# Attention weights times values: one F32 product on each column half of TensorE, in place of two split products

## The chip, the core and the metric

One core of a Trainium2 chip runs the whole kernel. Its engines work side by side and wait for each other on semaphores: PE (TensorE, the matrix unit; PEld is its loading of the stationary operand), DVE (VectorE), ACT (ScalarE), POOL (GpSimd), SP (SyncE, which issues most transfers) and the DMA engines. The metric is the device time of one execution in microseconds, the median of several runs.

## The reference, cut to what matters

The layer has three token mixers; the change touches the first, sparse attention with 8 heads of 64 in 2 groups, over 512 tokens in blocks of 128. With 8 blocks of 64 tokens and a top-k of 16, every block is selected, so the "selected" and the "window" attention are both plain causal attention, each with its own keys and values. What is computed per query block, cut down:

```python
p_c = _masked_softmax(einsum('bqghd,bngd->bghqn', qblk, k_cmp), valid_c)
o_c = einsum('bghqn,bngd->bqghd', p_c, v_cmp)
...
p_s = _masked_softmax(einsum('bqghd,bgqkd->bghqk', qblk, k_sel), valid_s)
o_s = einsum('bghqk,bgqkd->bqghd', p_s, v_sel)
...
p_w = _masked_softmax(einsum('bqghd,bkgd->bghqk', qblk, kwb), valid_w)
o_w = einsum('bghqk,bkgd->bqghd', p_w, vwb)
return gblk[..., 0:1] * o_c + gblk[..., 1:2] * o_s + gblk[..., 2:3] * o_w
```

The change is about the three products with the values, `o_c`, `o_s` and `o_w`.

## The kernel before, in words

Nearly all products run on float32r operands. No operand is used rounded alone; each is split in two: a high part (`wh`, `hH`, `ysH`, `ph`), which is the operand rounded to float32r by a copy, and a low part (`wl`, `hL`, `ysL`, `pl`), which is the rest and takes a subtraction. A full product is then three matmuls, high by high, high by low and low by high. `fm_block` and `tm_chunk` do this for the big projections: they load weights (`wr`), split them (`wh` on ACT in line 78, `wl` on DVE or POOL in line 79), and run three matmuls for each of 4 or 8 row blocks into a PSUM tile `mm_ps`. Every matmul is issued by the helper `mm` and so has line 62.

Attention is the loop over `ATT = (3, 2, 1, 0)`, the query blocks from the longest to the shortest. For each block `i` it makes compressed scores for the 8 heads (`sc_c`, softmax in `pcm`). Then for each group `g` of 4 heads:

- `o_ps`, one PSUM bank of 128 x 512, collects the output. It has one buffer (`BO = 1`).
- The compressed weights are transposed (`pc_ps`, line 836), spread over the four heads (`pd`, line 840, DVE), split into `ph` (line 843, ACT) and `pl` (line 844, DVE), and multiplied with `vcst`.
- For each of the two branches `b`: four heads of scores (`s_ps`), the row maximum (`mx`, line 858, DVE), the exponential (line 859, ACT), and the scaling of `P` (lines 865 and 867, on ACT, DVE or POOL). Then for each key tile `kt` up to `i`: four transposes of `P` into `p_ps` (line 872, two buffers), the split into `ph` (line 875, ACT) and `pl` (line 876, DVE), and two matmuls into `o_ps`.

The values are stationary. `vst` holds, side by side, the high part of the values in columns 0 to 63 and the low part in columns 64 to 127. So one matmul with `ph` and all 128 columns gives high by high in partitions 0 to 63 and high by low in partitions 64 to 127, and a second with `pl` and columns 0 to 63 adds low by high. Afterwards line 881 copies the lower half out (ACT), and line 885 adds both halves and puts the heads where the next stage wants them, `nsaY` (DVE, two instructions).

There are 40 such key tiles over all blocks, groups and branches (each of `i + 1` tiles, 2 groups, 2 branches) and 8 compressed products, 48 in all.

Instructions of each engine run in an order that the framework fixes when the program is built; it lays the work out on a simulated timeline, so an edit in one place can shift the order elsewhere. Between the steps of attention it puts the matmuls of `merge(1, ...)` and `merge(2, ...)`, which mix the other two branches into `macc` through `fm_block` (`mm_ps` from `ysH`, `ysL` or `hH`, `hL`). `HOLD` keeps the last four units of `merge(2, ...)` until certain products of attention are done (`anch`).

Of the kernel before, what the change touches and what calls it, by code (L numbers as in the profile page):

```python
# [9 lines left out]
F32 = mybir.dt.float32  # L10
R = mybir.dt.float32r
# [14 lines left out]
BS = 3  # L26
BO = 1
BP = 2
PS = "VVSG"
ATT = (3, 2, 1, 0)  # L30
HOLD = (-1,) * 12 + (3, 4, 5, 6)
# [9 lines left out]
def f(ap):  # L41
    return ap.bitcast(F32)
# [3 lines left out]
def hybrid_kernel(ctx, tc, x, p, norm_g, w_in, cmp_w1, cmp_w2, cmp_pe, sg_ln_g, sg_ln_b, sg_w, sg_b,  # L46
# [14 lines left out]
    def mm(o, a, b, start, stop, **kw):  # L61
        return PE.matmul(o, a, b, start=start, stop=stop, **kw).ins  # L62
# [173 lines left out]
    stp = st_ctx.enter_context(tc.tile_pool(name="stp", bufs=2))  # L236

    kcst = const.tile([128, 2, 2, 32], R, name="kcst")
    vcst = const.tile([128, 2, 128], R, name="vcst")
    hm = const.tile([128, 4], F32, name="hm")  # L240
    G.memset(hm, 0.0)
    for hh in range(4):
        G.memset(hm[32 * hh:32 * hh + 32, hh:hh + 1], 1.0)
    cp_ctx = ExitStack()
    cpp = cp_ctx.enter_context(tc.tile_pool(name="cpp", bufs=1))
    cps = cp_ctx.enter_context(tc.tile_pool(name="cps", bufs=1, space=PSUM))
# [60 lines left out]
    for kv in range(2):  # L307
        slp = slp2[:, kv * 64:kv * 64 + 64]
        sl = cpp.tile([128, 2, 4, 32], F32, tag=f"sl{kv}", name="sl")
        if kv == 0:  # L310
            sl = sl[:, 0, 0:2, :].rearrange("p g n -> p (g n)")
            V.tensor_copy(sl, slp)
            pk = cps.tile([128, 64], F32, tag="pk", name="pk")
            mm(pk, w2t[:, 0, :], sl, True, True)
            pk2 = pk.rearrange("p (g n) -> p g n", g=2)
            S.activation(kcst[:, :, 0, :], pk2, AF.Copy, scale=0.5)
            V.scalar_tensor_tensor(kcst[:, :, 1, :], pk2, 0.5, f(kcst[:, :, 0, :]), op0=OP.mult, op1=OP.subtract)
        else:
            V.tensor_copy(sl, slp.rearrange("p (g n) -> p g n", g=2).unsqueeze(2).to_broadcast([128, 2, 4, 32]))
            for g in range(2):  # L320
                pk = cps.tile([128, 64], F32, tag="pk", name="pk")
                mm(pk, sl[:, g].rearrange("p a n -> p (a n)"), w2t[:, 1, 0:64], True, True)
                S.activation(vcst[:, g, 0:64], pk, AF.Copy, scale=0.5)
                V.scalar_tensor_tensor(vcst[:, g, 64:128], pk, 0.5, f(vcst[:, g, 0:64]),
                                       op0=OP.mult, op1=OP.subtract)


    sh_ctx = ExitStack()
# [397 lines left out]
    nsa = nsa_ctx.enter_context(tc.tile_pool(name="nsa", bufs=1, side="right"))  # L726
    qst = nsa.tile([128, 4, 2, 512], R, name="qst")
    kst = [nsa.tile([128, 2, 2, 512], R, name=f"kst{b}") for b in range(2)]
    vst = nsa.tile([128, 4, 2, 2, 128], R, name="vst")
    nanch = []  # L730
    gate = nsa.tile([128, 4, 24], F32, name="gate")

# [1 line left out]

    def ev_v(t, ps):
        pv = ps[:, 0:256].rearrange("p (b g d) -> p b g d", b=2, g=2)
        S.copy(vst[:, t, :, :, 0:64], pv)
        V.tensor_tensor(vst[:, t, :, :, 64:128], pv, f(vst[:, t, :, :, 0:64]), OP.subtract)
        a_ = S.activation(gate[:, t, :], ps[:, 256:280], AF.Tanh, scale=0.5).ins
        nanch.append((a_, V.tensor_scalar(gate[:, t, :], gate[:, t, :], 0.5, 0.5, op0=OP.mult, op1=OP.add).ins))  # L740
    tm_chunk([(w_in, O_NVS, 128), (w_in, O_NVW, 152)], hH, hL, 8, ev_v)
# [69 lines left out]
    for i in ATT:  # L811
        isl = slice(i * 128, (i + 1) * 128)
        W = (i + 1) * 128
        sc = aps.tile([128, 8, 64], F32, tag="pt", name="sc_c", bufs=BP)
        for h in range(8):
            mm(sc[:, h, :], qst[:, h // 2, h % 2, isl], kcst[:, h // 4].rearrange("p a n -> p (a n)"), True, True)
        pcm = ap_.tile([128, 8, 32], F32, tag="pcm", name="pcm")
        mx8 = ap_.tile([128, 8], F32, tag="mx8", name="mx8")
        sm8 = ap_.tile([128, 8], F32, tag="sm8", name="sm8")
        V.tensor_tensor(pcm, sc[:, :, 0:32], cmask[:, i:i + 1, :].to_broadcast([128, 8, 32]), OP.add)  # L820
        V.tensor_tensor(pcm, sc[:, :, 32:64], pcm, OP.add)
        V.tensor_reduce(mx8, pcm, axis=AX.X, op=OP.max)
        V.tensor_tensor(pcm, pcm, mx8.unsqueeze(2).to_broadcast([128, 8, 32]), OP.subtract)
        S.activation(pcm, pcm, AF.Exp)
        V.tensor_reduce(sm8, pcm, axis=AX.X, op=OP.add)
        V.reciprocal(sm8, sm8)
        gv = gate[:, i, :].rearrange("p (h b) -> p b h", b=3)
        if i == 0:
            V.scalar_tensor_tensor(sm8, sm8, rowm, gv[:, 0, :], op0=OP.mult, op1=OP.mult)
        else:  # L830
            V.tensor_tensor(sm8, sm8, gv[:, 0, :], OP.mult)
        V.tensor_tensor(pcm, pcm, sm8.unsqueeze(2).to_broadcast([128, 8, 32]), OP.mult)
        for g in range(2):
            o_ps = aps.tile([128, 512], F32, tag="o", name="o_ps", bufs=BO)
            pc_ps = aps.tile([128, 128], F32, tag="pt", name="pc_ps", bufs=BP)
            PE.transpose(pc_ps, pcm[:, 4 * g:4 * g + 4, :].rearrange("p h n -> p (h n)"), ident)
            pd = ap_.tile([128, 4, 128], F32, tag="pd", name="pd", bufs=1)
            ph = ap_.tile([128, 512], R, tag="ph", name="ph", bufs=3)
            pl = ap_.tile([128, 512], R, tag="pl", name="pl", bufs=3)
            V.tensor_tensor(pd, pc_ps.unsqueeze(1).to_broadcast([128, 4, 128]),  # L840
                            hm.unsqueeze(2).to_broadcast([128, 4, 128]), OP.mult)
            pd2 = pd.rearrange("p h t -> p (h t)")
            S.copy(ph, pd2)
            V.tensor_tensor(pl, pd2, f(ph), OP.subtract)
            mm(o_ps, vcst[:, g, :], ph, True, False)
            mm(o_ps[0:64], vcst[:, g, 0:64], pl, False, False)
            for b in range(2):
                P = ap_.tile([128, 4, 512], F32, tag="P", name="P")
                mx = ap_.tile([128, 4], F32, tag="mx", name="mx")
                sm = ap_.tile([128, 4], F32, tag="sm", name="sm")  # L850
                for hh in range(4):
                    h = g * 4 + hh
                    s_ps = aps.tile([128, 512], F32, tag="s", name="s_ps", bufs=BS)
                    qs = qst[:, h // 2, h % 2, isl]
                    mm(s_ps[:, :W], qs, kst[b][:, g, 0, :W], True, False)
                    mm(s_ps[:, :W], qs, kst[b][:, g, 1, :W], False, False)
                    mm(s_ps[:, i * 128:W], identb, trib, False, True)
                    V.tensor_reduce(mx[:, hh:hh + 1], s_ps[:, :W], axis=AX.X, op=OP.max, negate=True)  # L858
                    S.activation(P[:, hh, :W], s_ps[:, :W], AF.Exp, bias=mx[:, hh:hh + 1],  # L859
                                 accum_out=sm[:, hh:hh + 1])  # L860
                V.reciprocal(sm, sm)
                V.tensor_tensor(sm, sm, gv[:, 1 + b, g * 4:g * 4 + 4], OP.mult)
                for hh in range(4):
                    if PS[hh] == "S":
                        S.activation(P[:, hh, :W], P[:, hh, :W], AF.Copy, scale=sm[:, hh:hh + 1])
                    else:
                        (G if PS[hh] == "G" else V).tensor_scalar(P[:, hh, :W], P[:, hh, :W], sm[:, hh:hh + 1],
                                                                  None, op0=OP.mult)
                for kt in range(i + 1):
                    p_ps = aps.tile([128, 512], F32, tag="pt", name="p_ps", bufs=BP)  # L870
                    for hh in range(4):
                        PE.transpose(p_ps[:, hh * 128:hh * 128 + 128], P[:, hh, kt * 128:kt * 128 + 128], ident)  # L872
                    ph = ap_.tile([128, 512], R, tag="ph", name="ph", bufs=3)
                    pl = ap_.tile([128, 512], R, tag="pl", name="pl", bufs=3)
                    S.copy(ph, p_ps)  # L875
                    V.tensor_tensor(pl, p_ps, f(ph), OP.subtract)  # L876
                    mm(o_ps[0:64], vst[:, kt, b, g, 0:64], pl, False, False)
                    last = mm(o_ps, vst[:, kt, b, g, :], ph, False, b == 1 and kt == i)
            anch.append(last)
            ot = ap_.tile([64, 512], F32, tag="ot", name="ot", bufs=1)  # L880
            S.copy(ot, o_ps[64:128])
            o4 = o_ps.rearrange("p (a e t) -> p a e t", a=2, e=2)
            t4 = ot.rearrange("p (a e t) -> p a e t", a=2, e=2)
            for e in range(2):
                V.tensor_tensor(nsaY[e * 64:e * 64 + 64, 2 * g:2 * g + 2, isl], o4[0:64, :, e, :], t4[:, :, e, :],
                                OP.add)
    at_ctx.close()
    nsa_ctx.close()

# [118 lines left out]
```

## Time and profile before

| | us |
|---|---|
| median of 3 runs (745.38 to 746.82) | 745.41 |
| the profiled execution | 747.35 |
| its span (first to last instruction) | 745.6 |
| PE busy in the span | 716.0 |
| DVE, ACT, POOL busy | 407.6, 354.2, 288.2 |
| attention with the merges in between, 395.6 to 566.3 | 170.7 |

The page of the profile has busy time by engine, the span in 40 slices (each digit the busy share in tenths, the row PEclk the clock that TensorE was granted), the DMA queues, the chain of work that ended last, and the costliest groups of instructions. A group reads: line, engine, operation, what is written from what, its shape, its count, busy time and mean, then idle time before it with what ended that. Matmuls overlap in a pipeline, so a recorded length is longer than the step from one start to the next; what a matmul costs the engine is read from the starts.

### The profile page before, as it was taken

Reading aid. Unit: us, or ns where it says so; the run is one execution under the profiler, and the core shown is the slowest. Engines: PE = TensorE matmul, PEld = TensorE weight load, DVE = VectorE, ACT = ScalarE, POOL = GpSimd, SP = SyncE. Lnnn points to the kernel's source line nnn. Section 1 sums busy time; section 2 is a strip of 40 time slices with the busy share of each in tenths; the row PEclk is TensorE's granted clock in tenths of the full one; section 3 lists DMA queues with packets and bytes.
Section 4 is the critical chain, followed back from the end, with each engine's and each line's share of the span. In section 5 each row is a group of like instructions: output and inputs, shape, how many; then the busy total and the mean of one; then the engine's idle time right before and its main releaser. Section 6 shows DMA issues by size and latency. Waiting matters only on the chain.

```text
span 745.6 us, 13074 instructions
## 1 busy us (share of the span) xinstructions
PE 716.0 (96%) x4941; PEld 606.6 (81%) x4941; DVE 407.6 (55%) x775; ACT 354.2 (48%) x743; POOL 288.2 (39%) x276
## 2 busy tenths in 40 slices
PE   4899999999999999999999999989999999999995
PEld 4788788999878987779877778767877888998995
DVE  6531587758933773645676565397554222226345
ACT  6554555542372332234565554576554333227453
POOL 6444740120220272300144345323445565256563
PEclk9999999999999999999999999999999999999998
DMA  6853122124546364336433212201228333132212
GB/s 200 182 136 100 48 80 71 44 87 140 156 113 215 101 172 124 107 115 203 135 94 105 57 44 70 71 16 42 54 60 267 100 89 124 58 113 72 78 64 114
DMA packets 106689, 78.73 MB, mean 106 GB/s; under 512 B 5569, under 2 KB 97282, under 8 KB 106626
## 3 DMA queue, kind: packets, MB, share of 16 engines
q1 hardware_dynamic: 105890, 75.27, 35.1%
q10 hardware_dynamic: 736, 2.63, 0.9%
q8 instruction: 39, 0.64, 0.4%
q14 instruction: 24, 0.20, 0.1%
HBM read 67.91 MB, written 9.96 MB: 104 GB/s over the span
## 4 chain that ended last, share of the span: by engine, by line
PE 87%; DVE 5%; ACT 2%; issue 2%; DMA 1%; POOL 1%; SPq 1%; ACTq 0%; POOLq 0%; DVEq 0%
PE mm_ps L62 69%; PE s_ps L62 3%; PE o_ps L62 2%; PE g_ps L62 2%; PE p_ps L872 2%; DMA w1t<-in_cmp_w_dram 1%; PE Yp L62 1%; PE r_ps L62 1%; DVE mx L858 1%; PE st_ps L62 1%; PE mx_ps L62 1%; DVE pl L876 1%; PE u_ps L62 1%; PE bk_ps L477 1%; ACT wh L78 1%
## 5 line engine op out<-in xcount | busy, mean ns | idle before, releaser
L79 POOL TENSOR_TENSOR wl<-wr,wh 128x512 fp32r<-128x512 f32 x144 | 192.5, 1345 | 276.5 <-ACT wh L78 255.5
L78 ACT CAST wh<-wr 128x512 fp32r<-128x512 f32 (+1 forms) x194 | 119.4, 620 | 169.6 <-PE mm_ps L62 117.6
L62 PE MATMUL mm_ps<-hH,wh 128*128 128x512 f32 (+1 forms) x440 | 174.2, 396 | 3.8 <-ACT kc L265 2.3
L62 PE MATMUL mm_ps<-hL,wh 128*128 128x512 f32 (+1 forms) x440 | 171.1, 389 | 0.0
L62 PE MATMUL mm_ps<-hH,wl 128*128 128x512 f32 (+1 forms) x440 | 170.7, 388 | 0.4 <-DVE wl L79 0.4
L62 PEld LDWEIGHTS mm_ps<-hH,wh 128*128 128x128 f32 x440 | 82.9, 188 | 21.3 <-ACT kc L265 2.5
L62 PEld LDWEIGHTS mm_ps<-hH,wl 128*128 128x128 f32 x440 | 82.7, 188 | 18.0 <-DVE wl L79 0.6
L62 PEld LDWEIGHTS mm_ps<-hL,wh 128*128 128x128 f32 x440 | 83.0, 189 | 16.5 <-issue 0.2
L62 PE MATMUL mm_ps<-wh,hL 128*128 128x256 f32 (+1 forms) x224 | 64.9, 290 | 0.0
L62 PE MATMUL mm_ps<-wh,hH 128*128 128x256 f32 (+1 forms) x224 | 63.8, 286 | 0.0
L62 PE MATMUL mm_ps<-wl,hH 128*128 128x256 f32 (+1 forms) x224 | 63.6, 285 | 0.0
L79 DVE TENSOR_TENSOR wl<-wr,wh 128x512 fp32r<-128x512 f32 (+1 forms) x50 | 38.0, 769 | 25.2 <-ACT wh L78 25.1
L62 PEld LDWEIGHTS mm_ps<-wh,hL 128*128 128x128 f32 x224 | 42.2, 188 | 1.1 <-issue 0.5
L62 PEld LDWEIGHTS mm_ps<-wh,hH 128*128 128x128 f32 x224 | 42.0, 188 | 1.2 <-issue 0.5
L62 PEld LDWEIGHTS mm_ps<-wl,hH 128*128 128x128 f32 x224 | 42.2, 188 | 0.5
L876 DVE TENSOR_TENSOR pl<-p_ps,ph 128x512 fp32r<-128x512 f32 x40 | 27.2, 685 | 25.9 <-ACT ph L875 25.9
L62 PE MATMUL mm_ps<-ysH,wh 128*128 128x512 f32 x96 | 38.6, 402 | 0.1
L62 PE MATMUL mm_ps<-ysL,wh 128*128 128x512 f32 x96 | 38.4, 400 | 0.2 <-DVE ysL L722 0.2
L62 PE MATMUL mm_ps<-ysH,wl 128*128 128x512 f32 x96 | 38.2, 398 | 0.0
L859 ACT ACTIVATE P<-s_ps,mx 128x512 f32<-128x512 f32 (+3 forms) x64 | 33.4, 532 | 7.9 <-DVE mx L858 5.5
L62 PE MATMUL mm_ps<-wh,mH 128*128 128x256 f32 x128 | 36.1, 286 | 0.6 <-DVE x L921 0.6
L62 PE MATMUL mm_ps<-wl,hT 128*128 128x256 f32 x128 | 35.9, 281 | 0.0
(336 smaller groups left out, 1437.6 us busy)
## 6 DMA issues: line engine op xcount, KB each, us to landing
wr<-in_w_in_dram SPq DMA_DIRECT2D x130, 256.0 KB
wr<-in_w_branch_dram SPq DMA_DIRECT2D x24, 256.0 KB
wr<-in_w_o_dram SPq DMA_DIRECT2D x16, 256.0 KB
wr<-in_w_ple_gate_dram SPq DMA_DIRECT2D x16, 256.0 KB
xs__129<-in_x_dram SPq DMA_DIRECT2D x4, 512.0 KB
w1t<-in_cmp_w_dram SPq DMA_DIRECT2D x4, 512.0 KB
x<-in_x_dram ACTq DMA_DIRECT2D x4, 512.0 KB
out_dram<-x SPq DMA_DIRECT2D x8, 256.0 KB
```

What stands on the lines that cost most here:

```text
L62: return PE.matmul(o, a, b, start=start, stop=stop, **kw).ins
L78: S.copy(h[:, :m], raw[:, :m])
L79: ph_["l"].tensor_tensor(l[:, :m], raw[:, :m], f(h[:, :m]), OP.subtract)
L477: PE.transpose(ps[:, c - c0, :], bk[:, c, 0:2].rearrange("p s t -> p (s t)"), ident)
L858: V.tensor_reduce(mx[:, hh:hh + 1], s_ps[:, :W], axis=AX.X, op=OP.max, negate=True)
L859: S.activation(P[:, hh, :W], s_ps[:, :W], AF.Exp, bias=mx[:, hh:hh + 1], accum_out=sm[:, hh:hh + 1])
L872: PE.transpose(p_ps[:, hh * 128:hh * 128 + 128], P[:, hh, kt * 128:kt * 128 + 128], ident)
L876: V.tensor_tensor(pl, p_ps, f(ph), OP.subtract)
```

## The change

The products with the values are made in F32 in place of float32r. `vst` and `vcst` keep the unsplit values, 64 columns wide, and the low part is no longer computed. The transposed weights are copied out of PSUM once, unsplit (`pt`), by ACT for even and DVE for odd key tiles (for block 0 by branch); `pd` is used as it stands. A product becomes two F32 matmuls of 64 stationary columns by 256 moving columns: `e = 0` writes partitions 0 to 63 of `o_ps` from columns 0 to 255, `e = 1` partitions 64 to 127 from columns 256 to 511. The transposes put the heads in the order 0, 2, 1, 3 (`hm` likewise), so that `o_ps` already has the layout of `nsaY`, and one ACT copy takes it out. `P` has three buffers in place of two, and `pt` and `pd` share four.

```diff
+BQ = 3
+BT = 4
...
-    vcst = const.tile([128, 2, 128], R, name="vcst")
+    vcst = const.tile([128, 2, 64], F32, name="vcst")
...
-        G.memset(hm[32 * hh:32 * hh + 32, hh:hh + 1], 1.0)
+        j = hh % 2 * 2 + hh // 2
+        G.memset(hm[32 * hh:32 * hh + 32, j:j + 1], 1.0)
...
-                S.activation(vcst[:, g, 0:64], pk, AF.Copy, scale=0.5)
-                V.scalar_tensor_tensor(vcst[:, g, 64:128], pk, 0.5, f(vcst[:, g, 0:64]),
-                                       op0=OP.mult, op1=OP.subtract)
+                S.activation(vcst[:, g, :], pk, AF.Copy, scale=0.5)
...
-    vst = nsa.tile([128, 4, 2, 2, 128], R, name="vst")
+    vst = nsa.tile([128, 4, 2, 2, 64], F32, name="vst")
...
-        S.copy(vst[:, t, :, :, 0:64], pv)
-        V.tensor_tensor(vst[:, t, :, :, 64:128], pv, f(vst[:, t, :, :, 0:64]), OP.subtract)
+        S.copy(vst[:, t], pv)
...
-            o_ps = aps.tile([128, 512], F32, tag="o", name="o_ps", bufs=BO)
+
+            o_ps = aps.tile([128, 2, 128], F32, tag="o", name="o_ps", bufs=BO)
+            first = [True]
+
+            def o_add(v, pt, done):
+                for e in range(2):
+                    q = mm(o_ps[e * 64:e * 64 + 64].rearrange("p a t -> p (a t)"), v, pt[:, e * 256:e * 256 + 256],
+                           first[0], done, skip_group_check=True)
+                first[0] = False
+                return q
...
-            pd = ap_.tile([128, 4, 128], F32, tag="pd", name="pd", bufs=1)
-            ph = ap_.tile([128, 512], R, tag="ph", name="ph", bufs=3)
-            pl = ap_.tile([128, 512], R, tag="pl", name="pl", bufs=3)
+            pd = ap_.tile([128, 4, 128], F32, tag="pt", name="pd", bufs=BT)
...
-            pd2 = pd.rearrange("p h t -> p (h t)")
-            S.copy(ph, pd2)
-            V.tensor_tensor(pl, pd2, f(ph), OP.subtract)
-            mm(o_ps, vcst[:, g, :], ph, True, False)
-            mm(o_ps[0:64], vcst[:, g, 0:64], pl, False, False)
+            o_add(vcst[:, g, :], pd.rearrange("p h t -> p (h t)"), False)
...
-                P = ap_.tile([128, 4, 512], F32, tag="P", name="P")
+                P = ap_.tile([128, 4, 512], F32, tag="P", name="P", bufs=BQ)
...
-                        PE.transpose(p_ps[:, hh * 128:hh * 128 + 128], P[:, hh, kt * 128:kt * 128 + 128], ident)
-                    ph = ap_.tile([128, 512], R, tag="ph", name="ph", bufs=3)
-                    pl = ap_.tile([128, 512], R, tag="pl", name="pl", bufs=3)
-                    S.copy(ph, p_ps)
-                    V.tensor_tensor(pl, p_ps, f(ph), OP.subtract)
-                    mm(o_ps[0:64], vst[:, kt, b, g, 0:64], pl, False, False)
-                    last = mm(o_ps, vst[:, kt, b, g, :], ph, False, b == 1 and kt == i)
+                        j = hh % 2 * 2 + hh // 2
+                        PE.transpose(p_ps[:, j * 128:j * 128 + 128], P[:, hh, kt * 128:kt * 128 + 128], ident)
+                    pt = ap_.tile([128, 512], F32, tag="pt", name="pt", bufs=BT)
+                    if (kt + (i == 0) * b) % 2:
+                        V.tensor_copy(pt, p_ps)
+                    else:
+                        S.copy(pt, p_ps)
+                    last = o_add(vst[:, kt, b, g, :], pt, b == 1 and kt == i)
             anch.append(last)
-            ot = ap_.tile([64, 512], F32, tag="ot", name="ot", bufs=1)
-            S.copy(ot, o_ps[64:128])
...
-            for e in range(2):
-                V.tensor_tensor(nsaY[e * 64:e * 64 + 64, 2 * g:2 * g + 2, isl], o4[0:64, :, e, :], t4[:, :, e, :],
-                                OP.add)
+            S.copy(nsaY[:, 2 * g:2 * g + 2, isl], o_ps)
```

The order on PE changes with it. Over the whole of attention the 96 new matmuls into `o_ps` stand in 42 stretches with no other matmul in them: 36 of one product (x2) and 6 of two (x4). Behind 34 of the stretches come transposes (`p_ps` or `pc_ps`), behind 8 another matmul; 9 have transposes in front of them.

The first place is the first products of block 3, where the compressed product and the first key tile stand. On PE before:

```order
L872 MATMUL p_ps<-ident,P 128x128 x4
L62 MATMUL o_ps<-ph,vcst 128x512
...
L62 MATMUL mm_ps<-ysL,wh 128x512
L62 MATMUL o_ps<-pl,vcst 64x512
L62 MATMUL mm_ps<-ysH,wl 128x512
L62 MATMUL mm_ps<-ysH,wh 128x512
L62 MATMUL o_ps<-pl,vst 64x512
L62 MATMUL o_ps<-ph,vst 128x512
L872 MATMUL p_ps<-ident,P 128x128 x4
```

And on PE with the change, at the same place:

```order
L64 MATMUL mm_ps<-ysL,wh 128x512
L64 MATMUL mm_ps<-ysH,wl 128x512
L64 MATMUL o_ps<-pd,vcst 64x256 x2
L64 MATMUL o_ps<-pt,vst 64x256 x2
L876 MATMUL p_ps<-ident,P 128x128 x8
L64 MATMUL s_ps<-kst_3734,qst 128x512 x2
```

The compressed product and the first key tile now stand together, and the transposes of two key tiles follow at once.

The second place is block 0, group 0. On PE before, the high and the low product with `vcst` stand back to back, behind short score matmuls:

```order
L62 MATMUL s_ps<-kst_3737,qst 128x128 x2
L62 LDWEIGHTS identb
L62 MATMUL s_ps<-trib,identb 128x128
L62 MATMUL o_ps<-ph,vcst 128x512
L62 MATMUL o_ps<-pl,vcst 64x512
L62 MATMUL o_ps<-pl,vst 64x512
L62 MATMUL o_ps<-ph,vst 128x512
L836 MATMUL pc_ps<-ident,pcm 128x128
```

And on PE with the change:

```order
L64 MATMUL mm_ps<-ysH,wh 128x512
L64 MATMUL mm_ps<-ysL,wh 128x512
L64 MATMUL mm_ps<-ysH,wl 128x512
L64 MATMUL o_ps<-pd,vcst 64x256 x2
L64 MATMUL o_ps<-pt,vst 64x256 x2
L876 MATMUL p_ps<-ident,P 128x128 x4
L845 MATMUL pc_ps<-ident,pcm 128x128
L64 MATMUL s_ps<-kst_3735,qst 128x128 x2
```

Here matmuls of the merge moved in front of the products, where scores stood before.

## Rows read from the trace of the kernel before

**Rows 1.** Page: busy time, share of the span and instructions by engine.
```profile
PE 716.0 (96%) x4941; PEld 606.6 (81%) x4941; DVE 407.6 (55%) x775; ACT 354.2 (48%) x743; POOL 288.2 (39%) x276
```

**Rows 2.** Stretches: length, busy PE, PEld, DVE, ACT, POOL (counts), clock, DMA.
```profile
540.00:551.00 11.00, 9.47 (x48) 7.58 (x47) 7.15 (x17) 7.00 (x22) 4.85 (x4) 0.84 0.25 69
...
395.60:566.30 170.70, 165.29 (x866) 130.94 (x865) 105.96 (x228) 94.88 (x232) 72.25 (x58) 0.99 0.22 61
```

**Rows 3.** Waits of PE in attention: total us, times, longest.
```profile
PE o_ps L62 <- DVE pl L844: 2.1, 2, 1.2
PE o_ps L62 <- DVE nsaY L885: 0.8, 1, 0.8
...
PE o_ps L62 <- DVE pl L876: 0.7, 2, 0.4
PE o_ps L62 <- ACT ph L843: 0.5, 1, 0.5
```

**Rows 4.** Timeline of PE at 544: start, length, instruction, idle before it.
```profile
544.53 0.48 PE L62 MATMUL o_ps<-ph,vcst 128*128 128x512 f32 x1
546.20 0.45 PE L62 MATMUL o_ps<-pl,vcst 128*64 128x512 f32 x1 [1.18 <-DVE pl L844]
```

**Rows 5.** Timeline of PE at 406, one key tile.
```profile
406.96 0.39 PE L62 MATMUL o_ps<-pl,vst 128*64 128x512 f32 x1
407.19 0.39 PE L62 MATMUL o_ps<-ph,vst 128*128 128x512 f32 x1
407.42 0.60 PE L872 MATMUL p_ps<-ident,P 128*128 128x128 f32 x4
407.78 0.48 PE L62 MATMUL mm_ps<-hH,wh 128*128 128x512 f32 x1
408.09 0.40 PE L62 MATMUL mm_ps<-hL,wh 128*128 128x512 f32 x1
```

**Rows 6.** Timeline of PE at 275, an F32 matmul with 256 columns on all 128.
```profile
275.63 0.59 PE L62 MATMUL mx_ps<-vn,wsT 128*128 128x256 f32 x2
275.87 0.58 PE L62 MATMUL mm_ps<-hH,wh 128*128 128x512 f32 x1
276.29 0.40 PE L62 MATMUL mm_ps<-hL,wh 128*128 128x512 f32 x1
```

**Rows 7.** Timeline of PE at 243, F32 matmuls alternating between the column halves.
```profile
243.43 0.28 PE L62 MATMUL mm_ps<-wh,hH 128*128 128x256 f32 x1
243.54 0.28 PE L62 MATMUL mm_ps<-wl,hH 128*128 128x256 f32 x1
243.75 0.69 PE L62 MATMUL r_ps<-SV,Gt 128*64 128x64 f32 x16
```

**Rows 8.** Timeline of PE, then PEld, at 36: one F32 matmul on one half.
```profile
35.86 0.40 PE L62 MATMUL mm_ps<-hH,wl 128*128 128x512 f32 x1
36.18 0.43 PE L62 MATMUL hid<-w1t,blk 128*64 128x128 f32 x2
36.55 0.49 PE L62 MATMUL mm_ps<-hH,wh 128*128 128x512 f32 x1
36.88 0.39 PE L62 MATMUL mm_ps<-hL,wh 128*128 128x512 f32 x1
...
36.54 0.19 PEld L62 LDWEIGHTS mm_ps<-hH,wh 128*128 128x128 f32 x1 [0.17 <-issue]
```

**Rows 9.** Tile views: count, shortest/median/longest ns, first and last start.
```profile
L62 PE MATMUL hid<-w1t,blk x64: 272/273/323, 36.2 to 42.6; 128*64 128x128 f32 x64
...
L872 PE MATMUL p_ps<-ident,P x160: 270/272/330, 395.8 to 557.4; 128*128 128x128 f32 x160
...
L62 PE MATMUL r_ps<-SV,Gt x128: 222/222/369, 213.2 to 323.2; 128*64 128x64 f32 x128
```

**Rows 10.** Groups of DVE in attention: busy us, mean ns, idle before.
```profile
L876 DVE TENSOR_TENSOR pl<-p_ps,ph 128x512 fp32r<-128x512 f32 x40 | 27.2, 685 | 25.9 <-ACT ph L875 25.9
...
L885 DVE TENSOR_TENSOR nsaY<-o_ps,ot 64x256 f32<-64x256 f32 x16 | 6.6, 414 | 1.3 <-ACT ot L881 1.2
```

More of the change, by code (lines that the diff above doesn't have):

```diff
@@ L871, in hybrid_kernel @@
                     for hh in range(4):
-                        PE.transpose(p_ps[:, hh * 128:hh * 128 + 128], P[:, hh, kt * 128:kt * 128 + 128], ident)
-                    ph = ap_.tile([128, 512], R, tag="ph", name="ph", bufs=3)
-                    pl = ap_.tile([128, 512], R, tag="pl", name="pl", bufs=3)
-                    S.copy(ph, p_ps)
-                    V.tensor_tensor(pl, p_ps, f(ph), OP.subtract)
-                    mm(o_ps[0:64], vst[:, kt, b, g, 0:64], pl, False, False)
-                    last = mm(o_ps, vst[:, kt, b, g, :], ph, False, b == 1 and kt == i)
-            anch.append(last)
-            ot = ap_.tile([64, 512], F32, tag="ot", name="ot", bufs=1)
-            S.copy(ot, o_ps[64:128])
-            o4 = o_ps.rearrange("p (a e t) -> p a e t", a=2, e=2)
-            t4 = ot.rearrange("p (a e t) -> p a e t", a=2, e=2)
-            for e in range(2):
-                V.tensor_tensor(nsaY[e * 64:e * 64 + 64, 2 * g:2 * g + 2, isl], o4[0:64, :, e, :], t4[:, :, e, :],
-                                OP.add)
+                        j = hh % 2 * 2 + hh // 2
[6 more added lines that the diff above has]
+                    last = o_add(vst[:, kt, b, g, :], pt, b == 1 and kt == i)
+            anch.append(last)
+            S.copy(nsaY[:, 2 * g:2 * g + 2, isl], o_ps)
     at_ctx.close()
```

## The prediction

> **What bounds the kernel now.** I read the page first. PE is busy for 716.0 of 745.6 us, 96%, and DVE, ACT and POOL for 55%, 48% and 39% [rows 1]. So the kernel is as long as PE's stream of matmuls, and an edit counts by what it adds to that stream or by the waits of PE that it takes away. Then I looked at the stretch that the change touches, 395.6 to 566.3. There PE is busy for 165.29 of 170.70 us, DVE for 105.96 and ACT for 94.88 [rows 2]: PE idles 5.4 us, the other two have a third of the stretch and more to spare. The waits of PE say where the idle time is: 2.1 + 0.7 us on `pl`, 0.5 us on `ph`, 0.8 us on the DVE instruction that empties the one `o_ps` bank, 4.1 us together [rows 3]. One of them is at 544.53, where the high product with `vcst` is issued and the low one has to wait until 546.20 for DVE [rows 4]. Around it the granted clock is 0.84 as a mean over 11 us [rows 2], that is, TensorE ran part of it at 1.2 GHz in place of 2.4, after it had idled. That costs 0.16 x 11 = 1.8 us. The most that the change can give back on PE in this stretch is therefore 5.4 + 1.8 = 7.2 us.
>
> **What a product costs PE before.** `pl` starts at 406.96, `ph` at 407.19, the transposes at 407.42 [rows 5]: 0.23 us a step, 0.46 us a product, and the transposes start without a gap. 48 products (40 key tiles, 8 compressed) are 48 x 0.46 = 22.1 us.
>
> **What a product costs PE after.** It is two F32 matmuls, and each shows as two passes. Four things have to be priced.
>
> *The passes.* An F32 matmul with 256 columns on the whole array is two records. From its start at 275.63 to the second matmul behind it at 276.29 are 0.66 us; 0.23 of that belongs to the matmul between, so two passes take 0.43 us, 0.215 each [rows 6]. The new product has four such passes, 0.86 us one after the other, which would be dear. But two of them go to columns 0 to 63 of the array and two to columns 64 to 127, and the trace has such pairs. `r_ps` alternates between the two halves: 16 passes of 64 columns between its first start and its last end, 0.69 us [rows 7]. A pass is recorded with 0.222 us [rows 9], so the first and the last start lie 0.47 us apart. Less 0.05 us for the first weights (next paragraph) that is 0.42 us, seven steps of 0.06 for eight pairs. By the 0.215 us for 256 columns one pass of 64 needs 0.054 us. So the two halves run side by side, and a new product takes 2 x 0.215 = 0.43 us, 0.03 less than before. Over 48 products that gives back 1.4 us.
>
> *Going in.* Before `r_ps` a matmul of 256 columns starts at 243.54, with steps of 0.12 us in front of it (243.43 to 243.54). The next should start at 243.66 and starts at 243.75 [rows 7], 0.09 us late. At 36 it is the same: 35.86 + 0.23 = 36.09, but `hid`, an F32 matmul on one half, starts at 36.18 [rows 8]. On top of this the first pass lasts 323 ns in place of 273 [rows 9], because its weights were not loaded ahead: 0.05 us. Behind a full-array matmul this is 0.14 us a stretch.
>
> *Coming out.* The `hid` pair at 36.18 works until about 36.18 + 0.05 + 2 x 0.107 = 36.45 (0.107 being half of 0.215). The next weights start to load at 36.54, 0.09 us later, and the matmul behind the next one starts at 36.88, 0.33 us after 36.55 and not 0.23: another 0.10 us for weights that could not load ahead [rows 8]. If transposes follow, their first record is up to 330 ns long in place of 272 [rows 9], so 0.06 us in place of 0.10.
>
> *How often.* The new order has 42 stretches of such products: 34 with transposes behind them, 8 with another matmul; 9 have transposes in front. There the weights of whatever comes next load in the open anyway (`mm_ps` behind the transposes starts at 407.78 and the next at 408.09, 0.31 in place of 0.23 [rows 5]), so I take 0.05 us off for each of these 9. The sum on PE:
>
> - 42 x (0.09 + 0.05 + 0.09) = 9.7 us for going in and coming out
> - 34 x 0.06 + 8 x 0.10 = 2.8 us for the weights behind
> - 9 x 0.05 = 0.5 us less
> - 48 x 0.03 = 1.4 us less
>
> That is **+10.6 us** on an engine that has no room. This price is the heart of the forecast, and the trace also has a row on the other side. The old `pl` matmul uses 64 stationary columns too, and it costs no gap on either side [rows 5]. So 64 columns by themselves cost nothing; the gaps stand at F32 matmuls that are laid on one half or the other. The new products are of that kind, F32 and with outputs in partitions 64 to 127, so I take the price of `hid` and `r_ps`. The lower bound is that of `pl`, no price: -1.4 us. The Trainium skill has a rule that speaks against this change (TensorEngine Tiling (Array Packing), "Key Properties"): a change of the tiling mode drains the engine. It gives no time for it; by it the first rival below is out, and the trace agrees with it at `hid` and `r_ps` alone, since the 64 columns of `pl` show no gap.
>
> **What DVE and ACT lose.** DVE loses 40 subtractions `pl` of 685 ns, 27.2 us, and 16 additions into `nsaY`, 6.6 us [rows 10], besides 8 subtractions behind `pd`. It gains 18 of the 40 copies `pt`. The trace has no plain DVE copy of this shape; the bound from above is the 685 ns of the subtraction that reads the same tile, from below nothing, and near the upper end it is 18 x 0.6 = 11 us. ACT keeps 22 of 40 copies and the copy out of `o_ps`. Both engines are off the path, so none of this is a gain by itself. It is one only through the waits of PE. The path from transposes to product gets shorter by the subtraction, and from `pd` to product by a copy and a subtraction. The bank is emptied by one ACT copy in place of a copy and two additions of 414 ns. And at the second place shown in the order, the product with `vcst` no longer has a DVE subtraction to wait for and stands behind merge matmuls. So I take all four waits as gone, 4.1 us, and the slow clock with them, 1.8 us, since it came after such a wait: **-5.9 us**. The bounds are 0 (new waits of the same length appear on `pt` and `pd`) and -7.2 us. The edits to `vst` and `vcst` are before the stretch, on DVE, which is busy for 55% of the span; I cost them at nothing. If DVE were what PE waits for there, they would give back less than 2 us.
>
> **The sum.** +10.6 - 5.9 = +4.7 us. The profiled execution took 747.35 us (span 745.6), 0.26% over the median of the three runs, so I put the difference on the median: 745.41 + 4.7 = **750.1 us**, 0.6% slower. Its own range is 745.41 + 10.6 - 7.2 = 748.8 to 745.41 + 10.6 = 756.0.
>
> **The rivals.**
>
> *No price for the halves.* The new products go through without gaps, as `pl` does. Then PE gains 1.4 us, and the waits 5.9: 745.41 - 7.3 = 738.1 us, faster. For it: 40 rows of `pl` without a gap. Against it: every stretch of F32 work on a half that I looked at (`hid`, `r_ps`) has the gap on both sides. It decides as soon as the price of a stretch is under 0.17 us ((5.9 + 1.4) / 42) and not 0.29. 11%.
>
> *Half the price.* Going in or coming out is partly hidden, for example because the halves drain while the transposes load. At 6 us for the 42 stretches it is 745.41 + 6 - 1.4 - 5.9 = 744.1, within or just past what can be told. 13%.
>
> *One behind the other.* The four passes run in program order, half 0 twice and then half 1 twice, and the second half can't start before the last pass of the first. A lone product then needs three steps in place of two, 0.215 us more, 48 x 0.215 = 10.3 us: 760.4 us. `r_ps` speaks against it: done that way its first pass would stand alone, the last start would be eight steps behind the first, 0.05 + 8 x 0.06 = 0.53 us, and it is 0.47. 7%. The Trainium skill has such a rule (TensorE: Matmul & The Clock Gate, "The mechanism" under packing small matmuls): matmuls start and end strictly in program order. By that rule the time would be the 760.4 us of this rival; the trace so far agrees better with the other reading.
>
> *New waits.* The order was laid out again, and the transposes of two key tiles now follow each other with two `p_ps` buffers. If copies on ACT stand behind exponentials and PE waits as long as before, the 5.9 us are not given back: 756.0 us; with a few waits more, 758. 12%.
>
> **Chances.** The forecast 57%, no price 11%, half the price 13%, one behind the other 7%, new waits 12%. A run of this kernel can be told from no change at about 0.2%, 1.5 us. Faster by more: 11% + half of the 13% = 17%. Same: the other half and a little of the forecast's lower end, 8%. Slower: 75%. For the range I leave out the no-price case below and the one-behind-the-other case above, and what lies beyond 758: 742 to 758.
>
> **What would show it.** In the changed profile each `o_ps` stretch should show its first start 0.09 us late, four records in two steps of 0.215 us, and 0.09 us before the next weights. PE in the attention stretch should be about 5 us longer, with waits on `pl` gone and DVE some 29 us less busy. If the records follow each other in three steps, the third rival holds; if the weights of `o_ps` load during the matmul in front, the first. The forecast is wrong if the stretch shows the gaps and is not longer: then PE had more waits to give back than the 7.2 us counted here.

## The result: slower by more than forecast, and the profile after

The changed kernel takes 757.52 us (median of 6 runs, 755.97 to 759.18), the kernel before 746.76 us beside it (6 runs, 745.38 to 748.38). The ratio is 1.014, interval 1.012 to 1.016: +10.8 us, where the forecast was +4.7. The profiled execution took 758.18 us with a span of 756.5, against 747.35 and 745.6 before. Executions of one kernel differ by up to 3 us. Part of that lies outside the change: in 300 to 350 us the granted clock is 0.93 in one profile, 0.97 or 1.00 in another. So where two traces are compared, I use the stretch from the first score matmul of attention (`sc_c`) to the first matmul with `w_o`: 271.67 us before (356.69 to 628.36), 281.43 us after (357.58 to 639.01), +9.76.

The page's busy row, to compare with [rows 1]:

```profile
PE 726.7 (96%) x5037; PEld 601.1 (79%) x5037; DVE 383.0 (51%) x723; ACT 338.8 (45%) x717; POOL 287.8 (38%) x276
```

PE is 10.7 us busier, DVE 24.6 us less. Now the stretch that the change touches, the window around the old clock dip (both stand in [rows 2]), and two windows behind attention, with the same columns:

```profile
395.60:566.30 170.70, 170.70 (x956) 121.47 (x955) 82.88 (x182) 79.24 (x206) 71.43 (x57) 1.00 0.22 61
...
540.00:551.00 11.00, 11.00 (x67) 8.84 (x66) 5.13 (x14) 4.48 (x15) 5.09 (x5) 1.00 0.27 71
566.00:574.00 8.00, 4.30 (x19) 3.16 (x17) 1.37 (x2) 1.76 (x3) 2.73 (x3) 1.00 1.01 350
574.00:580.00 6.00, 3.83 (x9) 2.96 (x10) 2.68 (x4) 1.74 (x3) 0.00 (x0) 0.52 0.37 119
```

Inside attention PE is busy all the time at full clock: every wait of [rows 3] and the dip are gone. The new thing stands behind: PE busy for 4.30 of 8 us while the DMA engines are full, then a clock of 0.52, close to the lower of TensorE's two levels (1.2 of 2.4 GHz), after PE had idled for 5.9 us. All waits of PE from 395 to 600:

```profile
PE mm_ps L64 <- ACT ysH L722: 5.9, 1, 5.9
PE mm_ps L64 <- ACT sg L795: 0.3, 1, 0.3
```

The products themselves, first on PE, then on PEld, at the first place of the order (in the timeline x4 counts records; a product is four):

```profile
401.65 0.40 PE L64 MATMUL mm_ps<-ysH,wl 128*128 128x512 f32 x1
401.98 0.65 PE L64 MATMUL o_ps<-pd,vcst 128*64 128x256 f32 x4
402.46 0.60 PE L64 MATMUL o_ps<-pt,vst 128*64 128x256 f32 x4
403.00 1.09 PE L876 MATMUL p_ps<-ident,P 128*128 128x128 f32 x8
```

```profile
401.42 0.19 PEld L64 LDWEIGHTS mm_ps<-ysH,wl 128*128 128x128 f32 x1
401.98 0.20 PEld L64 LDWEIGHTS o_ps<-pd,vcst 128*64 128x64 f32 x4 [0.37 <-issue]
...
402.99 0.86 PEld L876 LDWEIGHTS p_ps<-ident,P 128*128 128x128 f32 x8 [0.38 <-issue]
```

401.65 + 0.23 = 401.88, but the product starts at 401.98, 0.10 late. Its weights load at that moment, 0.37 us after the loader fell idle, and not in advance. The first product takes 0.48 us, the second 0.54 until the transposes. The old pair took 0.46 with no gap [rows 5].

The wait behind attention, in the chain of work that ended last (start, length, what):

```profile
557.72 2.99 DMA zs<-dr_nz
...
562.08 3.71 DMA zs<-dr_nz
...
566.70 7.97 DMA zs<-dr_nz
...
574.70 0.70 DVE nsaY L895
...
575.49 0.64 ACT ysH L722
...
576.17 3.84 PE mm_ps L64 x8
```

`zs` is a gate that lies in DRAM. It is multiplied into the output of attention `nsaY`, and the product is split into `ysH` and `ysL`, with which `merge(0, ...)` starts. The third load takes 7.97 us, the two before it 2.99 and 3.71. What lies in its way is the prefetch of `x` and `fg`, 2.5 MB for a much later step, issued by ACT. ACT's and SP's queues with the change:

```profile
563.25 0.37 ACTq L905 DMA_DIRECT2D x<-in_x_dram  x1
563.65 1.44 ACTq L905 DMA_DIRECT2D x<-in_x_dram  x3
566.70 0.98 SPq L894 DMA_DIRECT2D zs<-dr_nz  x2
566.71 0.34 ACTq L906 DMA_DIRECT2D fg<-in_final_norm_g_dram  x1
```

And the same in the kernel before:

```profile
563.64 0.81 SPq L896 DMA_DIRECT2D zs<-dr_nz  x2
566.44 0.84 ACTq L907 DMA_DIRECT2D x<-in_x_dram  x2
567.36 1.12 ACTq L907 DMA_DIRECT2D x<-in_x_dram  x2
568.52 0.47 ACTq L908 DMA_DIRECT2D fg<-in_final_norm_g_dram  x1
```

Before, all of `zs` was issued ahead of `x`. Now four loads of `x` are issued ahead of the last two of `zs`, and the DMA share is 1.01. The Trainium skill (DMA: Bandwidth & Descriptors, "Queues, rings and completion order") says that ACT's and SP's transfers share the same 16 engines, and that the signal of a finished transfer lands behind every earlier write of its engine, of other queues too. The 7.97 us agree with that; no run here separates it from plain sharing.

After the wait TensorE is slow for some 5 us more, as the starts of the matmuls show:

```profile
576.17 0.79 PE L64 MATMUL mm_ps<-ysH,wh 128*128 128x512 f32 x1 [5.87 <-ACT ysH L722]
576.76 0.69 PE L64 MATMUL mm_ps<-hH,wh 128*128 128x512 f32 x1
...
581.09 0.40 PE L64 MATMUL mm_ps<-hL,wh 128*128 128x512 f32 x1
```

From 576.17 to 581.09 are 11 matmuls in 4.92 us, where 11 steps of 0.23 are 2.5: the half clock costs 2.4 us. The matmuls on `hH` behind the late one do not use `zs`; they only stand behind it in PE's order.

### The profile page after: what moved, and what is told of

The parts are those of the page before. It is cut to its first block, busy times and chain, and to the rows that moved or that the text cites. A ratio compares the mean times of both kernels' runs of the same rounds, so it can differ in the third digit from the quotient of the medians.

```text
span 756.5 us, 13173 instructions
## 1 busy us (share of the span) xinstructions
PE 726.7 (96%) x5037; PEld 601.1 (79%) x5037; DVE 383.0 (51%) x723; ACT 338.8 (45%) x717; POOL 287.8 (38%) x276
## 4 chain that ended last, share of the span: by engine, by line
PE 88%; DMA 3%; DVE 3%; ACT 2%; issue 1%; POOL 1%; SPq 1%; POOLq 0%; ACTq 0%; DVEq 0%
PE mm_ps L64 68%; PE s_ps L64 3%; PE o_ps L64 3%; PE p_ps L876 3%; PE g_ps L64 2%; DMA zs<-dr_nz 2%; DMA w1t<-in_cmp_w_dram 1%; PE Yp L64 1%; PE u_ps L64 1%; PE r_ps L64 1%; PE st_ps L64 1%; PE mx_ps L64 1%; PE bk_ps L478 1%; PE hid L64 0%; PE bo L64 0%
## 5 line engine op out<-in xcount | busy, mean ns | idle before, releaser
L862 ACT ACTIVATE P<-s_ps,mx 128x512 f32<-128x512 f32 (+3 forms) x64 | 33.5, 528 | 28.0 <-DVE mx L861 21.9
L861 DVE TENSOR_REDUCE mx<-s_ps 128x1 f32<-128x512 f32 (+3 forms) x64 | 29.6, 484 | 12.9 <-PE s_ps L64 12.8
```

## The experiments

Theory: two separate costs. First, PE pays by stretch of F32 products for going in and out of the column halves, less the waits given back, as in the forecast. Second, and not in the forecast, the prefetch that now goes first delays `zs`. Rivals: F32 by itself is the dear thing, or the wait behind attention comes from something else. All ratios are to the kernel before on the same chip (medians 747.4 to 748.0). The edits are cut down to what matters.

### e1: the prefetch behind the loads of zs

```diff
-    for t in range(4):
-        S.dma_start(x1[:, t, :], x[t * 128:(t + 1) * 128, :])
-    S.dma_start(fg, ...)
+    with tc.issue_after(ylast):        # ylast: the ACT half of the last y0 split
+        for t in range(4):
+            S.dma_start(x1[:, t, :], x[t * 128:(t + 1) * 128, :])
+        S.dma_start(fg, ...)
```

> The changed kernel with one edit: the loads of x and fg are queued on ACT behind the last high part ysH of the y0 split, so that they come after the loads of zs. Theory (the prefetch fills the DMA engines and delays the last zs, and PE waits for that): the 5.9 us wait of PE for ysH behind attention shrinks to under 2 us, the half clock after it goes (about 2 us), the time falls from 757.5 to 750 us (749 to 752). Rival (zs is late because its buffers come free late, the prefetch only runs beside it): the wait stays at 5 to 6 us and the time at 757 us.

Measured: 751.35 us, ratio 1.0042 (1.0024 to 1.0059). `x` is now issued from 572.03 on. All waits of PE from 395 to 600:

```profile
PE mm_ps L64 <- ACT ysH L722: 0.5, 1, 0.5
PE mm_ps L64 <- DVE ysL L723: 0.2, 1, 0.2
PE mm_ps L64 <- DVE sg L802: 0.2, 1, 0.2
```

The stretch from `sc_c` to `w_o` is 274.08 us, 7.35 less than with the change. All of it lies behind attention: from `sc_c` to the last product with the values the two traces take the same time (205.2 us), and the loads of `zs` are issued at the same distance from `sc_c`. The waits account for 6.2 - 0.9 = 5.3 us (5.9 + 0.3, less 0.5 + 0.2 + 0.2) and the half clock, which is gone (1.00 in 560 to 600), for 2.4. Together that is 0.3 more than the 7.35, which was not placed.

### e9: the loads of zs ahead, the prefetch left alone

```diff
-        zs = gp.tile([128, 512], F32, tag="sg", name="zs")
+        zs = zq.tile([128, 512], F32, tag="zq", name="zs")   # four buffers of their own
```

> The changed kernel with the prefetch of x and fg left where the change has it, but the four loads of zs get four buffers of their own and so are issued together, ahead of x. It is the other way to take the collision away. Theory (the last zs landed behind the prefetch): the 5.9 us wait for ysH goes to under 1 us, 749.5 to 751.5 us, as e1 (751.35). Rival (e1 won because ACT had the x loads out of its way, not because zs landed sooner): 755 to 758 us.

Measured: 752.25 us, ratio 1.0061 (1.0038 to 1.0084); the stretch is 273.89 us. The waits of PE behind attention are 0.6 and 0.3 us. The four `zs` are now issued from 562.85 to 564.70, beside `x` (from 562.94) and not behind it. So e1 takes the wait away with the loads of `zs` where they were, e9 with the first three of `x` where they were (the fourth moves from 564.62 to 566.86, behind `zs`): the wait hangs on how the two stand to each other. How much of e9 is due to the bytes and how much to the earlier issue, it doesn't tell apart.

### e2: the same order forced on the kernel before

```diff
+    # x and fg issued by SP here, fgl the last of them
     for q in range(4):
         zs = gp.tile([128, 512], F32, tag="sg", name="zs")
-        SY.dma_start(zs, dr["nz"][q * 128:(q + 1) * 128, :])
+        if q >= 2: (issue_after fgl)
+        SY.dma_start(zs, dr["nz"][q * 128:(q + 1) * 128, :])
```

> The kernel before with one edit: the loads of x and fg are issued by SP in front of the last two loads of zs. Theory (that order alone costs the wait, whatever attention is like): zs lands 6 to 9 us later, PE gets a wait of 4 to 7 us behind attention with a slow clock after it, 746.8 becomes 752 to 755 us. Rival (the wait needs the new attention): no new wait above 1 us, 746 to 748 us.

Measured: 760.86 us, ratio 1.0175 (1.0152 to 1.0199). The cost is there with the old attention, but twice what I expected. SP's queue, then PE:

```profile
568.89 2.04 SPq L902 DMA_DIRECT2D x<-in_x_dram  x4
570.97 0.53 SPq L903 DMA_DIRECT2D fg<-in_final_norm_g_dram  x1
571.54 1.58 SPq L909 DMA_DIRECT2D zs<-dr_nz  x2
```

```profile
581.36 0.79 PE L62 MATMUL mm_ps<-ysH,wh 128*128 128x512 f32 x1 [11.25 <-ACT ysH L721]
```

On one queue the last `zs` are issued at 571.54 in place of 563.64. This trace reaches `sc_c` 2.1 us later than the one before (358.79), so they lose 5.8 us by their issue alone. I had counted only the sharing. So e2 shows that the order costs time whatever attention is like; its size is not that of the change.

### e3: F32 on the whole array

```diff
-                for e in range(2):
-                    q = mm(o_ps[e * 64:e * 64 + 64]..., v, pt[:, e * 256:e * 256 + 256], ...)
+                q = mm(o_ps, v.rearrange("p g d -> p (g d)"), pt, first[0], done)
```

> As e1, but each product with the values is one F32 matmul on the whole array: 128 stationary columns (the values of both groups, of whose results one half is used) by 512 moving columns, in place of two 64 x 256 on the column halves. Theory (going in and out of the column halves costs 0.29 us a stretch, F32 by itself nothing): a product takes 0.86 us in place of 0.43, plus 20.6 us, and 12 us of gaps go: about 8.6 us over e1, 758 to 760 us, weights of o_ps load during the matmul in front. Rival (the gaps belong to F32 matmuls, whatever columns they use): gaps stay, about 20 us over e1, 769 to 771 us.

Measured: 759.48 us, ratio 1.0143 (1.0117 to 1.0169), 8.1 over e1. PE, then PEld, at the first products:

```profile
398.75 0.39 PE L64 MATMUL mm_ps<-ysH,wl 128*128 128x512 f32 x1
398.98 1.02 PE L64 MATMUL o_ps<-pd,vcst 128*128 128x512 f32 x2
399.84 1.02 PE L64 MATMUL o_ps<-pt,vst 128*128 128x512 f32 x2
400.70 0.49 PE L875 MATMUL p_ps<-ident,P 128*128 128x128 f32 x3
```

```profile
398.76 0.42 PEld L64 LDWEIGHTS o_ps<-pd,vcst 128*128 128x128 f32 x2
```

A product takes 0.86 us, and there is no gap: 398.75 + 0.23 = 398.98, the weights load while the matmul in front runs, and the transposes follow after 0.86. So the gaps belong to the column halves and not to F32 by itself. That rival falls. (F32 with 64 stationary columns and the column halves always go together here; no run separates these two.)

### e7, e4, e8: the same products in fewer stretches

All three build on e1. The products wait for the last copy `pt` of two key tiles (e7), of a branch, with the compressed product (e4), or of a whole group (e8). e4 has six buffers for `pt`, e8 nine and two for `P`. The dependency is added to each product:

```diff
-                    last = o_add(vst[:, kt, b, g, :], pt, b == 1 and kt == i)
+                    todo.append((kt, pt))
+                    if len(todo) == 2 or kt == i:      # e4: kt == i; e8: b == 1 and kt == i
+                        for k2, p2 in todo:
+                            last = o_add(vst[:, k2, b, g, :], p2, b == 1 and k2 == i, cpy)
+                        todo = []
```

> As e1, but the products of two key tiles of a branch go one behind the other: 29 stretches of F32 products on halves. Theory (price by stretch): on the line from 42 stretches (751.35 us) to 16 (743.58 us), that is 747.5 us, 746.5 to 748.5. Rival (e4 won by putting the compressed product later or by holding products back, not by the count): 750 to 752 us, PE busy as in e1.

> As e1, but the products of a group wait for the last pt of their branch and go one behind the other, the compressed product with them: 16 stretches of F32 products on halves in place of 42, with the same 96 matmuls. Theory (price by stretch, 0.23 us and 0.06 to 0.10 us for the weights behind): 26 x 0.29 = 7.5 us less on PE, 742 to 744 us if no wait is new, up to 746 with some. Rival (price by product, or no price and attention longer for another reason): PE busy as in e1, 750 us or more with the longer wait for pt.

> As e4, but the products of both branches of a group go one behind the other: 8 stretches; nine buffers for pt, two for P. Theory (price by stretch, 0.29 us): 8 x 0.29 = 2.3 us under e4, 741.3 us, with no new wait. Rival (the products now wait for the last copy of a group and nothing covers it): PE waits of 2 to 5 us on o_ps, 743 to 747 us.

| kernel | stretches | from their first start to the next matmul, sum us | `sc_c` to `w_o`, us | median us | ratio, interval |
|---|---|---|---|---|---|
| e1 | 42 | 27.1 | 274.08 | 751.35 | 1.0042 (1.0024 to 1.0059) |
| e7 | 29 | 25.1 | 273.79 | 748.93 | 1.0020 (1.0004 to 1.0037) |
| e4 | 16 | 23.1 | 267.27 | 743.58 | 0.9945 (0.9924 to 0.9967) |
| e8 | 8 | 21.9 | 265.77 | 742.60 | 0.9924 (0.9895 to 0.9953) |

The sums are added up from the starts of all stretches in each trace; going in and the weights behind are not in them. One stretch each of e4 and e8:

```profile
414.52 0.65 PE L64 MATMUL o_ps<-pd,vcst 128*64 128x256 f32 x4
415.00 1.90 PE L64 MATMUL o_ps<-pt,vst 128*64 128x256 f32 x16
416.83 1.09 PE L880 MATMUL p_ps<-ident,P 128*128 128x128 f32 x8
```

```profile
424.79 0.65 PE L64 MATMUL o_ps<-pd,vcst 128*64 128x256 f32 x4
425.28 3.62 PE L64 MATMUL o_ps<-pt,vst 128*64 128x256 f32 x32
428.83 1.09 PE L880 MATMUL p_ps<-ident,P 128*128 128x128 f32 x8
```

Behind the first product, four take 1.83 us and eight 3.55: (3.55 - 1.83) / 4 = 0.43 us a product inside a stretch, and 1.83 - 4 x 0.43 = 0.11 for coming out. By the medians a stretch costs 7.77 / 26 = 0.30 (e4) or 8.75 / 34 = 0.26 us (e8), by the traces 6.81 / 26 = 0.26 or 8.31 / 34 = 0.24. e7 missed its 747.5 by 1.4: its trace has a 2.3 us wait for `ysH` again (e1: 0.5) and a clock of 0.96 in 560 to 600, that is 1.8 + 1.6 us behind attention. Without them its trace has 270.4 us, where the line from e1 to e4 gives 270.7. e4 and e8 beat the kernel before.

### e5, e6: what took the waits inside attention away

e5 is e1 with `BQ = 2` in place of 3. e6 is the kernel before with `bufs=3` for `P` and `bufs=2` for `ph` and `pl`.

> As e1 (prefetch late, 751.35 us, 42 stretches), with two buffers for P in place of three. It asks what took PE's waits inside attention away. Theory (the shorter chains did: no split between copy and product, one copy to empty o_ps): no change, 750 to 752.5 us, waits of PE inside attention under 1.5 us. Rival (the third buffer of P did): the 4 to 7 us come back, 755 to 758 us.

> The kernel before with three buffers for P (and two each for ph and pl, for space), split products as they were. The same question from the other side. Theory (the waits on pl, ph and nsaY belong to the chains of the split product): they stay at 3 to 5 us and the time at 746 to 749 us. Rival (the third buffer of P takes them away): 741 to 743 us.

e5: 751.65 us, ratio 1.0053 (1.0032 to 1.0073), and no wait of PE inside attention (behind it one of 1.6 us on `ysH`). e6: 746.75 us, ratio 0.9982 (0.9966 to 0.9998), with these waits of PE:

```profile
PE o_ps L62 <- DVE pl L844: 1.4, 2, 0.9
PE o_ps L62 <- DVE pl L876: 0.8, 3, 0.4
PE o_ps L62 <- DVE nsaY L885: 0.8, 1, 0.8
...
PE o_ps L62 <- ACT ph L843: 0.5, 1, 0.5
```

3.5 us of the 4.1 in [rows 3] stay. The third buffer of `P` isn't what gave the waits back. The dip of the clock is another matter: this trace has none (1.00 in 395 to 566), though most of the waits are there.

### e10, e11: own buffers for zs, where they were not needed

The edit of e9, put on e8 and on the kernel before.

> As e8 (8 stretches, prefetch late, 742.6 us), with the four buffers for zs of e9. Theory: the 0.9 us wait for ysH that e8 still has goes, 741 to 742.5 us. Rival: the wait is covered or another takes its place, 742.6 us or more.

> The kernel before with the four buffers for zs alone. PE has no wait above 0.3 us behind attention there, so by the theory nothing changes: 746.5 to 748.5 us. If it gains 2 us or more, part of what e8 and e10 gain over the kernel before is not due to attention.

Both theories failed (for e10 the rival's 742.6 or more holds): 747.21 us, ratio 0.9999 (0.9983 to 1.0014), for e10, 754.0 us, ratio 1.0084 (1.0063 to 1.0105), for e11. SP's queue and PE in e10:

```profile
557.30 1.76 SPq L905 DMA_DIRECT2D zs<-dr_nz  x4
```

```profile
561.55 0.50 PE L64 MATMUL mm_ps<-ysH,wh 128*128 128x512 f32 x1 [4.29 <-ACT ysH L722]
```

The new buffers lie in space that attention gives up late: SP's own wait in front of these loads is for PE's `o_ps` products (1.9 us in both traces). The four loads start at 557.30, where e8 issued the first at 548.72; in e11 at 562.29, before at 555.34 (the second at 559.08). The first `zs` is then late too: PE waits 4.3 us in e10, 2.8 + 1.9 in e11. In e9 the four were issued at 562.85, late as well, but PE still had merge matmuls to do until 568.4; in e11 it had run out at 564.6. So the point is when `zs` lands and what PE has left to do by then, and own buffers are no remedy by themselves.

## Why the prediction was wrong

Some groups of attention have these rows, which the points below use; the first is of the kernel before:

```profile
L872 PE MATMUL p_ps<-ident,P 128*128 128x128 f32 x160 | 24.9, 273 | 0.5 <-DVE P L867 0.4
L876 PE MATMUL p_ps<-ident,P 128*128 128x128 f32 x160 | 25.7, 284 | 0.0
...
L881 ACT COPY pt<-p_ps 128x512 f32<-128x512 f32 x22 | 12.9, 586 | 23.2 <-PE p_ps L876 23.2
...
L879 DVE COPY pt<-p_ps 128x512 f32<-128x512 f32 x18 | 12.4, 692 | 46.1 <-PE p_ps L876 46.1
```

*Passes: right.* Two steps of 0.215 us were forecast for a product; inside a stretch it takes 0.43 us. The third rival, one behind the other, falls with its 760.4. The Trainium skill's sentence on strict order (TensorE: Matmul & The Clock Gate, "The mechanism") gave that rival; 0.43 for four passes of 0.215 shows that passes on the two halves run side by side, whatever order they start in.

*Going in, coming out: right.* 0.10, 0.05 and 0.11 us where I took 0.09, 0.05 and 0.09. The records of the 160 transposes have a mean of 284 ns, before 273: 160 x 0.011 = 1.8 us, or 0.05 for each of the 34 stretches with transposes behind, where I took 0.06. As a sum: 27.1 - 22.1 = 5.0 us more from first start to next matmul, 42 x 0.10 = 4.2 for going in, 1.8 for the transposes behind and about 0.6 for the weights behind the other 8 stretches, together 11.6 where the forecast was +10.6. Half of the difference is the 0.5 us that I took off for the 9 stretches with transposes in front: the starts show about the same 0.10 us going in there, so nothing was to be taken off. That the price is by stretch and belongs to the halves is shown by e3, e4 and e8, which came out within their forecasts or, for e8, 1.3 us over. "No price" and "half the price" fall. The rule of the Trainium skill (TensorEngine Tiling (Array Packing), "Key Properties") that a change of tiling mode drains the engine agrees; the runs add its size, 0.24 to 0.30 us for there and back.

*Waits given back: right in direction, too small in size.* -5.9 was taken with a bound of -7.2; inside attention all of that came. e5 and e6 show that the waits did not go by the third buffer of `P`; that leaves the shorter chains and the new order on PE, which no run separates. And 7.2 was no upper bound: a wait costs PE more than the idle time listed for it, since a matmul's record is longer than its step. At 544.53 [rows 4] 1.18 us are listed, but the next matmul starts 1.67 us later and not about 0.3, so 1.4 us are lost. Over the 12 idle gaps of PE in that stretch the starts give some 2 us more than the 5.4 us of idle time.

*So the forecast of the part that I looked at held:* without the prefetch in the way (e1) the kernel takes 751.35 us, for a forecast of 750.1 with a range of its own of 748.8 to 756.0. Against the kernel beside it that is +3.1 us for +4.7. In the traces the stretch grew by 2.4, where 11.6 - 7.2 + 0.7 (0.9 us of waits behind attention in e1, 0.2 before) would give 5.1. Of the 2.7 us between, some 2 are the waits' true cost, and about 1 lies in the old products: 0.46 us was read at one place, but behind short score matmuls they took 0.48 to 0.55 us (426.98 to 427.48, for one). Both are estimates from the starts in the trace before. DVE in the stretch of [rows 2] became 23.1 us less busy, not 29, which decided nothing.

*The step that failed: the sum had no term behind 566 us.* I costed ACT's part by its busy time ("Both engines are off the path, so none of this is a gain by itself") and asked what a new wait could be only inside attention, where the rival "New waits" put it (`p_ps`, copies behind exponentials, 12%). The wait came right behind attention. In the new order the four loads of `x` went ahead of the last two of `zs`; which part of the edit moved them was not tested. The price of the wait, 5.3 us of idle time and 2.4 us of half clock, is the 7.35 us between e1 and the changed kernel but for 0.3; the sum had nothing for it. The time fell into that rival's 756 to 758, and so into the range of 742 to 758, by another mechanism: that is luck. The order is fixed when the program is built, so where the loads stand on ACT and SP could have been compared before the run. What to weigh it by was at hand as well: 2.5 MB of `x` and `fg` and 0.5 MB of `zs` for the same engines, and no matmul for PE to go on with in front of the one that needs `ysH`.

## What to carry to other kernels

F32 products on column halves cost here what their passes cost, plus 0.24 to 0.30 us for each stretch of them; so keep them together, and count stretches and not products (8 stretches with the late prefetch are 0.8% faster than the split products, 42 with the early one 1.4% slower). When the order on an engine changes, follow its transfers too, past the end of the edited stretch: a prefetch that nobody waits for can push a transfer that everybody waits for. Buffers of one's own make a load early only if their space is free early.

## What was not expected of the hardware

A `zs` load of 256 KB took 2.6 to 3.6 us with no load of `x` beside it (e1) and 7.97 us with 2 MB issued ahead of it on another queue. A wait of 5.9 us on PE was followed by a clock near TensorE's lower level until about 581, which cost another 2.4 us. DVE's plain copy of a 128x512 tile out of PSUM takes 692 ns, ACT's 586, so the copy saves DVE nothing against the old subtraction's 685 [rows 10].
